# Second layer's modulation as VectorE row sums in the first feed-forward, in place of TensorE products in the recurrence

## The chip, the cores and the metric

One core of one Trainium2 chip. The time is device time in microseconds of one launch; its measurement for the kernel before is three runs, 1637.95, 1640.65 and 1649.41 us, median 1640.65 us.

Engines are called by the names of the profile: PE is TensorE (PEld its weight loads), DVE is VectorE, ACT is ScalarE, POOL is GpSimd, and SP is the engine whose queue issues most of the loads.

## The reference, cut to what matters

Two layers over 256 latent tokens of 1024 channels, with 256 context tokens beside them in the first layer. Each layer is half a feed-forward, a mixer, and half a feed-forward. All three are modulated: a vector `silu(c)` times a 1024 x 9216 matrix of the layer gives nine vectors of 1024 values, three (shift, scale, gate) for each of the three parts.

```python
m_lat = jnp.split((jax.nn.silu(c) @ ada_w[i] + ada_b[i])[:, None, :], N_MOD, axis=-1)
...
def half_ffn(h, m, off, g, w_gu, w_down):
    y = rmsnorm(h, g) * (1 + m[off + 1]) + m[off]
    return h + 0.5 * m[off + 2] * swiglu(y, w_gu, w_down)
...
h_lat = half_ffn(h_lat, m_lat, 0, norm_g[i, 0], ffn1_w_gu[i], ffn1_w_down[i])
y_lat = modulate(h_lat, norm_g[i, 1], m_lat[3], m_lat[4])
h_lat = h_lat + m_lat[5] * mixer(y_lat)
h_lat = half_ffn(h_lat, m_lat, 6, norm_g[i, 2], ffn2_w_gu[i], ffn2_w_down[i])
```

The first layer (i = 0) does the same for the context with `m_ctx` from `c_ctx`. Its mixer is RWKV-7, a recurrence over tokens with a 64 x 64 state for each of 12 heads and in both directions, beside a Fourier mixing of a quarter of the channels. The second layer's mixer is a gated depthwise convolution beside a pooling; the context takes no part in that layer.

## The kernel before, in words

**Tiles.** The tokens' state h lies with channels on partitions, as 8 tiles of 128 channels by 256 tokens for each stream. A weight of 128 x 1024 is loaded whole on SP's queue (tile `wraw`, 512 KB) and split into two parts, `whi` by ScalarE (L190) and `wlo` by VectorE (L191); each product is three matmuls (L195 to L197), high by high, high by low, low by high.

**Stages, in order.** The first feed-forward (`ffn`, both streams, 512 columns a product) runs until about 405 us: 22 slots in three parts of 8, 7 and 7, a slot being a gate and an up product of 8 x 3 matmuls each, the product of the two (`hd`, L433) and its low part (`hl`, L361). At a part's end come the 8 products of `down`, and after each the update of h. Gate and up products use four PSUM banks in turn, down products two. Then come the input projection of the mixer and its features, and from 551 us on the recurrence: three groups of four heads, for each group the generator `chain` with 8 steps of 64 tokens (four of the context, then four of the latent tokens, which also give outputs by L821 and L823). A step issues small products of 64 or 128 rows and columns, each waiting for the one before through VectorE, ScalarE or GpSimd. In between, six pieces at a time after each step (`PR[0]`), stands the work of the next group (`features`, `inverse`), or for the last group the Fourier mixing and most of the output projection (`project_most`). When that has run out, the chain's steps stand alone; this is from 605 us in the first group, from 743 in the second and from 872 in the third. After the recurrence follow three feed-forwards over the latent tokens alone and the second layer's mixer.

**The modulation of the first layer.** `ada_first` makes the first norm's columns on TensorE. All others, 56 columns of 128 values for the latent stream and 24 for the context, are row sums: `ada_job` loads two columns' weights, transposed, as a tile `adaw` of 128 x 2048 (L277, 1024 KB, on GpSimd's queue, three buffers), and VectorE multiplies it elementwise by `cb`, which holds silu(c) in every partition, and adds up along the free dimension in the same instruction (L281, `accum_out`). These jobs are a list of generators, and each slot of the first feed-forward, and each down product but the last part's last two, takes two steps of it (`jobs` = 2, 44 places in all); there are 60 steps.

**The modulation of the second layer.** `ada_wide` makes it on TensorE. Each of 18 blocks of 512 columns gets four loads of 512 KB on SP's queue, into the buffers of `wraw`, and eight matmuls with silu(c) as 32 stationary columns and 512 columns of weights (L260), four of them side by side in rows of 32 of one bank. Then a copy by ScalarE (`adas`, L265), four transposes (L268) and a reduction by VectorE (L269) into `mod[1, 0]`. The matmuls have a lowered priority for the scheduler (-200). In the recurrence, after each step of `chain`, 4, 5 or 4 pieces of this list are driven, by the group (`PR[1 + g]`). `mod[1, 0]` is read from the third feed-forward on.

**Order.** The order on each engine is made by a scheduler from the order of the program and these priorities; an engine runs its instructions in that order, and one that waits holds all behind it.

Of the kernel before, what the change touches and what calls it, by code (L numbers as in the profile page):

```python
# [7 lines left out]
F32 = mybir.dt.float32  # L8
F32R = mybir.dt.float32r
AF = mybir.ActivationFunctionType  # L10
ALU = mybir.AluOpType
# [36 lines left out]
def dft():  # L48
    """[bd(cos64) | bd(sin64)] / 128, then cos256 and -sin256 by tiles of rows."""
# [13 lines left out]
def pool_counts():  # L63
    """1 / tokens of the centred windows, by the widths of the four groups."""
    t = np.arange(T)
    z = np.zeros((P, 2, T), np.float32)
    for g, w in enumerate((2, 4, 8, 16)):
        n = np.minimum(t + w - 1 - w // 2, T - 1) - np.maximum(t - w // 2, 0) + 1
        z[g % 2 * CW:g % 2 * CW + CW, g // 2, :] = 1.0 / n
    return z  # L70
# [9 lines left out]
def lay_out(a):  # L80
    """Arrays of the launch: inputs re-laid so that every load is contiguous per partition."""
# [19 lines left out]
    d["adat"] = w[0].T.reshape(9 * KT // 2, 2, P, D)[KT:].transpose(0, 2, 1, 3)  # L101
    d["ada1"] = w[1].reshape(4, 2, P, 18, 512).transpose(3, 0, 2, 1, 4)
# [31 lines left out]
class Net:  # L134
# [76 lines left out]
    def ada_first(self, b, r, ab):  # L211
        """Shift and scale of channel tile b of the first norm, for both streams, into columns b of ab."""
# [20 lines left out]
    def ada_rows(self, pool, vecs):  # L233
        """silu(c) along the free dimension of every partition."""
# [13 lines left out]
    def ada_wide(self, b, pool):  # L248
        """Columns 512 b .. of the second layer's modulation, in pieces of four loads."""
        nc = self.nc  # L250
        ps = self.bank("ada")
        for q in range(4):
            w = self.wp.tile([P, KT, P], F32, tag="wraw", name=self.nm("wraw"), bufs=4)
            w = w.rearrange("p k c -> p (k c)").rearrange("p (k n) -> p k n", k=2)
            nc.sync.dma_start(w, self.ins["ada1"][b, q])
            for i in range(2):
                k = 2 * q + i
                g = k % 4
                with self.tc.high_priority(-200):
                    nc.tensor.matmul(ps[32 * g:32 * g + 32, :], lhsT=self.cs[:, k, :], rhs=w[:, i, :],  # L260
                                     start=k < 4, stop=k >= 4, tile_position=(0, 32 * g), skip_group_check=True)
                if i:
                    yield
        sb = self.mp.tile([P, 512], F32, tag="adas", name=self.nm("adas"), bufs=1)
        nc.scalar.copy(sb, ps)  # L265
        pt = self.bank("ada")
        for i in range(4):
            nc.tensor.transpose(pt[:, i * P:(i + 1) * P], sb[:, i * P:(i + 1) * P], self.ident)  # L268
        nc.vector.tensor_reduce(out=self.mod[1, 0][:, 4 * b:4 * b + 4], in_=pt.rearrange("p (b g v) -> p b v g", b=4, g=4)[:, :, 0, :],  # L269
                                axis=AX.X, op=ALU.add)  # L270
        yield

    def ada_job(self, blk, vecs):
        """Columns blk and blk + 1 of the first layer's modulation, as sums along the free dimension."""
        nc = self.nc
        w = self.ap.tile([P, KT, 256], F32, tag="ada0", name=self.nm("adaw"), bufs=3).rearrange("p (i a) b -> p i (a b)", i=2)
        nc.gpsimd.dma_start(w, self.ins["adat"][blk // 2 - KT])  # L277
        for i in range(2):
            for v in vecs:
                junk = self.ap.tile([P, D], F32, tag="adaj", name=self.nm("adaj"), bufs=1)  # L280
                nc.vector.scalar_tensor_tensor(out=junk, in0=w[:, i, :], scalar=1.0, in1=self.cb[v], op0=ALU.mult,  # L281
                                               op1=ALU.mult, accum_out=self.mod[0, v][:, blk + i:blk + i + 1])
# [5 lines left out]
    def modcol(self, l, v, m, scale=None, g=None):  # L288
        """Columns [P, KT] of modulation m; optionally scaled, or (1 + m) * g."""
# [1070 lines left out]
```

## Time and profile before

| | |
|---|---|
| median of three runs | 1640.65 us |
| the profiled execution (span) | 1651.6 us |
| PE busy | 1555.6 us, 94% |
| PEld busy | 1319.8 us, 80% |
| DVE busy | 1082.6 us, 66% |
| ACT busy | 677.3 us, 41% |
| POOL busy | 204.9 us, 12% |
| instructions | 29927 |
| moved by DMA | 253.40 MB |

The profiled execution has no other time than its span, and is one execution apart from the three runs. A share of busy time is a mean over stages that differ, so the views are read stage by stage: windows of time give each engine's busy time in a stretch, with the clock that TensorE was granted (1.00 is full speed) and the share of time in which the 16 DMA engines were busy; the chain of waits gives what the end of a stretch waited for, step by step; lines and timelines give single instructions.

### The profile page before, as it was taken

How to read it: one execution, taken by the hardware profiler on the slowest of the kernel's cores; microseconds unless marked ns; L12 is line 12 of the kernel's file. 1: busy time of each engine (PE TensorE's matmuls, PEld its weight loads, DVE VectorE, ACT ScalarE, POOL GpSimd, SP SyncE). 2: the span in 40 equal slices, each digit the busy share in tenths (PEclk: the TensorE clock that was granted, in tenths of full speed). 3: DMA queues.
4: the chain of work that ended last, by engine and by line, in shares of the span. 5: the costliest groups of instructions: out<-in, count | busy, mean ns of one | idle time of the engine just before them, and what ended most of it. 6: DMA issues, size and time to landing. Idle time of an engine off the chain costs nothing.

```text
span 1651.6 us, 29927 instructions
## 1 busy us (share of the span) xinstructions
PE 1555.6 (94%) x12102; PEld 1319.8 (80%) x12102; DVE 1082.6 (66%) x1994; ACT 677.3 (41%) x1101; POOL 204.9 (12%) x291
## 2 busy tenths in 40 slices
PE   5999999999989899899999899999999996899997
PEld 3788888888867655555587699999999985799997
DVE  4899954335689686466462577656776479767754
ACT  4431222223553542441441455444454355445442
POOL 0000100000040430330210100000000056300000
PEclk9999999999989789789995899999999997799999
DMA  9667943223222124444530355565556532435562
GB/s 370 230 242 257 346 136 103 95 84 123 77 65 96 56 93 151 158 170 148 191 104 14 116 180 186 175 187 179 181 182 176 167 102 89 141 130 185 181 177 95
DMA packets 68810, 253.40 MB, mean 153 GB/s; under 512 B 8032, under 2 KB 10864, under 8 KB 63936
## 3 DMA queue, kind: packets, MB, share of 16 engines
q1 hardware_dynamic: 64080, 219.46, 40.2%
q0 software_dynamic: 4592, 32.03, 5.4%
q8 instruction: 95, 1.56, 0.4%
q14 instruction: 43, 0.35, 0.1%
HBM read 249.36 MB, written 2.10 MB: 152 GB/s over the span
## 4 chain that ended last, share of the span: by engine, by line
PE 81%; DVE 13%; ACT 3%; issue 2%; POOL 1%; DMA 1%; SPq 0%; POOLq 0%; DVEq 0%; ACTq 0%
PE gu L195 13%; PE gu L196 13%; PE gu L197 13%; PE down L197 7%; PE down L195 7%; PE down L196 7%; PE ada L260 3%; PE mx L823 2%; PE mx L821 2%; DVE wlo L191 2%; DVE ocv L1022 1%; DVE oo L1022 1%; PE gu L1049 1%; PE pg L744 1%; PE down L802 1%
## 5 line engine op out<-in xcount | busy, mean ns | idle before, releaser
L190 ACT CAST whi<-wraw 128x1024 fp32r<-128x1024 f32 (+1 forms) x298 | 305.1, 1028 | 524.5 <-PE gu L196 224.0
L191 DVE TENSOR_TENSOR wlo<-wraw,whi 128x1024 fp32r<-128x1024 f32 (+1 forms) x298 | 356.6, 1199 | 154.0 <-ACT whi L190 146.4
L195 PE MATMUL gu<-yh,whi 128*128 128x258 f32 (+1 forms) x1408 | 438.4, 312 | 6.4 <-ACT yh L375 4.5
L196 PE MATMUL gu<-yl,whi 128*128 128x258 f32 (+1 forms) x1408 | 437.6, 311 | 0.0
L197 PE MATMUL gu<-yh,wlo 128*128 128x258 f32 (+1 forms) x1408 | 436.5, 310 | 0.2 <-DVE wlo L191 0.2
L195 PEld LDWEIGHTS gu<-yh,whi 128*128 128x128 f32 x1408 | 265.8, 189 | 24.2 <-ACT yh L375 5.7
L197 PEld LDWEIGHTS gu<-yh,wlo 128*128 128x128 f32 x1408 | 267.4, 190 | 15.2 <-DVE wlo L191 1.1
L196 PEld LDWEIGHTS gu<-yl,whi 128*128 128x128 f32 x1408 | 267.2, 190 | 14.8 <-DVE yl L377 0.9
L196 PE MATMUL down<-hl,whi 128*128 128x256 f32 (+1 forms) x704 | 217.3, 309 | 0.0
L195 PE MATMUL down<-hh,whi 128*128 128x256 f32 (+1 forms) x704 | 217.3, 309 | 0.0
L197 PE MATMUL down<-hh,wlo 128*128 128x256 f32 (+1 forms) x704 | 217.3, 309 | 0.0
L195 PEld LDWEIGHTS down<-hh,whi 128*128 128x128 f32 x704 | 134.4, 191 | 7.4
L197 PEld LDWEIGHTS down<-hh,wlo 128*128 128x128 f32 x704 | 134.4, 191 | 7.4
L196 PEld LDWEIGHTS down<-hl,whi 128*128 128x128 f32 x704 | 134.4, 191 | 7.3
L350 POOL TENSOR_TENSOR rs<-ms,mhalf 128x2 f32<-128x2 f32 (+1 forms) x9 | 10.9, 1209 | 822.8 <-DVE ms L347 822.8
L281 DVE SCALAR_TENSOR_TENSOR adaj<-adaw,cb 128x1024 f32<-128x1024 f32 x80 | 97.8, 1223 | 4.0 <-DMA adaw<-in_adat_dram 2.8
L260 PE MATMUL ada<-wraw,ccs 128*32 128x512 f32 x288 | 75.9, 669 | 1.0 <-DVE mod L269 1.0
L384 DVE SCALAR_TENSOR_TENSOR hlat<-down,mc,hlat 128x256 f32<-128x256 f32 x46 | 22.2, 483 | 62.9 <-PE down L197 62.9
L438 DVE COPY wb<-gu 128x1 f32<-128x1 f32 x132 | 20.3, 154 | 46.4 <-PE gu L197 46.4
L360 ACT CAST hh<-hd 128x256 fp32r<-128x256 f32 (+1 forms) x88 | 40.5, 461 | 23.9 <-DVE hd L433 13.1
L964 PE MATMUL gu<-yo,wraw 128*128 128x256 f32 x192 | 45.4, 396 | 1.9 <-ACT yo L375 1.9
L1006 POOL TENSOR_TENSOR opart<-opart,opr 128x256 f32<-128x256 f32 x54 | 45.2, 837 | 5.0 <-ACT opr L1004 1.2
(339 smaller groups left out, 2419.1 us busy)
## 6 DMA issues: line engine op xcount, KB each, us to landing
wraw<-in_gu_dram SPq DMA_DIRECT2D x176, 512.0 KB, 3.3
wraw<-in_ada_dram SPq DMA_DIRECT2D x72, 512.0 KB, 4.2
adaw<-in_adat_dram POOLq DMA_DIRECT2D x28, 1024.0 KB, 5.7
wraw<-in_down_dram SPq DMA_DIRECT2D x64, 448.0 KB, 3.3
wraw<-in_down_dram SPq DMA_DIRECT2D x32, 512.0 KB, 3.5
wraw<-in_win_dram SPq DMA_DIRECT2D x22, 512.0 KB, 3.5
wraw<-in_owin_dram SPq DMA_DIRECT2D x14, 512.0 KB, 3.6
ada<-in_ada_dram SPq DMA_DIRECT2D x4, 1024.0 KB, 16.8
```

The source lines that it names most:

```text
L190: nc.scalar.copy(hi[:, :k, :], raw[:, :k, :])
L191: (eng or nc.vector).tensor_tensor(out=lo[:, :k, :], in0=raw[:, :k, :], in1=hi[:, :k, :].bitcast(F32), op=ALU.subtract)
L195: mm(ps, lhsT=wh, rhs=xh, start=start, stop=False, **k)
L196: mm(ps, lhsT=wh, rhs=xl, start=False, stop=False, **k)
L197: mm(ps, lhsT=wl, rhs=xh, start=False, stop=stop, **k)
L260: nc.tensor.matmul(ps[32 * g:32 * g + 32, :], lhsT=self.cs[:, k, :], rhs=w[:, i, :], start=k < 4, stop=k >= 4, tile_position=(0, 32 * g), ...
L281: nc.vector.scalar_tensor_tensor(out=junk, in0=w[:, i, :], scalar=1.0, in1=self.cb[v], op0=ALU.mult, op1=ALU.mult, accum_out=self.mod[0, v ...
L360: self.nc.scalar.copy(hi, x)
L821: mm(p3[o:o + CW, x, :], lhsT=UV[:, x, hd, :], rhs=rv(S["RR"][:, hd, x, :]), start=True, stop=False, tile_position=(0, o), skip_group_chec ...
L823: mm(p3[o:o + CW, x, :], lhsT=Xs[lo, x, hd, :], rhs=rv(r), start=False, stop=True, tile_position=(0, o), skip_group_check=True)
L964: nc.tensor.matmul(ps[:, :n], lhsT=w[:, k, :], rhs=y[:, k, :], start=k == 0, stop=k == KT - 1)
L1006: nc.gpsimd.tensor_tensor(out=part, in0=prev, in1=pr, op=ALU.add)
```

## The change

The second layer's 72 columns are computed like the first layer's: 36 more jobs on the same list, for the latent stream alone, each a load of 1024 KB on GpSimd's queue and two row sums on VectorE. The list has 132 steps, and each of the 44 places takes three. `ada_wide` goes, and with it its loads, matmuls, copies, transposes and reductions and the driving of it in the recurrence. The launch lays out both layers' weights transposed in one array. The diff also drops docstrings and comments, which are left out here; lines move by 1 to 28 numbers.

```diff
-    d["adat"] = w[0].T.reshape(9 * KT // 2, 2, P, D)[KT:].transpose(0, 2, 1, 3)
-    d["ada1"] = w[1].reshape(4, 2, P, 18, 512).transpose(3, 0, 2, 1, 4)
+    d["adat"] = w.transpose(0, 2, 1).reshape(9 * KT, 2, P, D)[KT:].transpose(0, 2, 1, 3)
...
-    def ada_wide(self, b, pool):
...
-    def ada_job(self, blk, vecs):
+    def ada_job(self, l, blk, vecs):
         nc = self.nc
         w = self.ap.tile([P, KT, 256], F32, tag="ada0", name=self.nm("adaw"), bufs=3).rearrange("p (i a) b -> p i (a b)", i=2)
-        nc.gpsimd.dma_start(w, self.ins["adat"][blk // 2 - KT])
+        nc.gpsimd.dma_start(w, self.ins["adat"][l * 9 * KT // 2 + blk // 2 - KT])
         for i in range(2):
             for v in vecs:
                 junk = self.ap.tile([P, D], F32, tag="adaj", name=self.nm("adaj"), bufs=1)
                 nc.vector.scalar_tensor_tensor(out=junk, in0=w[:, i, :], scalar=1.0, in1=self.cb[v], op0=ALU.mult,
-                                               op1=ALU.mult, accum_out=self.mod[0, v][:, blk + i:blk + i + 1])
+                                               op1=ALU.mult, accum_out=self.mod[l, v][:, blk + i:blk + i + 1])
             yield
...
-PR = (6,4,5,4)
+PR = 6
...
-                    net.jobs += [net.ada_job(m * KT + k, (0, 1) if m < 5 else (0,)) for m in range(2, 9) for k in range(0, KT, 2)]
+                    net.jobs += [net.ada_job(0, m * KT + k, (0, 1) if m < 5 else (0,)) for m in range(2, 9) for k in range(0, KT, 2)]
+                    net.jobs += [net.ada_job(1, k, (0,)) for k in range(0, 9 * KT, 2)]
...
-                    net.ffn(0, h, yh, yl, gate, acc, fp, 2, start)
+                    net.ffn(0, h, yh, yl, gate, acc, fp, 3, start)
...
-            wide = [net.ada_wide(b, lp) for b in range(18)]
...
-                    drive(side, PR[0])
-                    drive(wide, PR[1 + g])
+                    drive(side, PR)
...
-            drive(wide, 1000)
```

The order on VectorE in the first feed-forward, between the fourth and the fifth gate product (`hd`) of the second part. Before:

```order
L433 TENSOR_TENSOR hd_1630<-sg_1629,gu_1604 128x512
L191 TENSOR_TENSOR wlo_1790<-wraw_1791,whi_1789 128x1024
L361 TENSOR_TENSOR hl_1338<-hd_1630,hh_1337 128x512
L191 TENSOR_TENSOR wlo_1821<-wraw_1822,whi_1820 128x1024
L433 TENSOR_TENSOR hd_1704<-sg_1703,gu_1678 128x512
```

The same place after (L407 is `hd`, L190 `wlo`, L335 `hl`, L255 a row sum, `mc` columns of the first layer's gate):

```order
L407 TENSOR_TENSOR hd_1690<-sg_1689,gu_1664 128x512
L190 TENSOR_TENSOR wlo_1860<-wraw_1861,whi_1859 128x1024
L335 TENSOR_TENSOR hl_1386<-hd_1690,hh_1385 128x512
L255 SCALAR_TENSOR_TENSOR adaj_1777,mod_77<-adaw_1775,cb 128x1024
L255 SCALAR_TENSOR_TENSOR adaj_1779,mod_77<-adaw_1775,cb 128x1024
L255 SCALAR_TENSOR_TENSOR adaj_1851,mod_77<-adaw_1849,cb 128x1024
L190 TENSOR_TENSOR wlo_1891<-wraw_1892,whi_1890 128x1024
L255 SCALAR_TENSOR_TENSOR adaj_1853,mod_77<-adaw_1849,cb 128x1024
L255 SCALAR_TENSOR_TENSOR adaj_1857,mod_77<-adaw_1855,cb 128x1024
L266 TENSOR_TENSOR mc_1876_10574<-mod_77,smallc 128x8
L255 SCALAR_TENSOR_TENSOR adaj_1933,mod_77<-adaw_1855,cb 128x1024
L407 TENSOR_TENSOR hd_1768<-sg_1767,gu_1742 128x512
```

Before, the row sums have ended by this place; after, six of them stand here, and such a run stands between most gate products until the fifth of the last part's seven, ahead of which the last row sum stands.

The order on TensorE in the recurrence, at the second latent step of the first group: L823 the last output product of the step before, L782, L791 and L730 (transposes of values) the step's own products, L260 and L268 the second layer's modulation. Before:

```order
L823 MATMUL mx_5589<-rs_5312,Xs_5510 64x64
L782 MATMUL down_5629<-XV_5281,AG_5543 64x64
L260 MATMUL ada_5238<-wraw_5489,ccs 32x512
L260 MATMUL ada_5238<-wraw_5493,ccs 32x512 x2
L782 MATMUL down_5629<-XV_5281,AG_5543 64x64 x7
L268 MATMUL ada_5499<-cst,adas_5497 128x128 x4
L791 MATMUL down_5640<-RH_5638,A_3316 64x64 x8
L730 MATMUL mx_5664<-cst,z_3298 128x128
```

The same place after (L797, L756, L704 and L765 are the lines 823, 782, 730 and 791 of before):

```order
L797 MATMUL mx_5705<-rs_5469,Xs_5646 64x64
L756 MATMUL down_5728<-XV_5438,AG_5679 64x64 x8
L704 MATMUL mx_5763<-cst,z_3514 128x128
L704 MATMUL mx_5763<-cst,vr_5765 128x128
L704 MATMUL mx_5763<-cst,z_3694 128x128
L704 MATMUL mx_5763<-cst,vr_5769 128x128
L765 MATMUL down_5739<-RH_5737,A_3532 64x64 x8
```

The modulation's products and transposes are gone from the step, and the transposes of values (L704) now stand ahead of the product by the inverse (L765) and not behind it.

## Rows read from the trace of the kernel before

**Rows 1.** The page: the chain that ended last, by line.

```profile
PE gu L195 13%; PE gu L196 13%; PE gu L197 13%; PE down L197 7%; PE down L195 7%; PE down L196 7%; PE ada L260 3%; PE mx L823 2%; PE mx L821 2%; DVE wlo L191 2%; DVE ocv L1022 1%; DVE oo L1022 1%; PE gu L1049 1%; PE pg L744 1%; PE down L802 1%
```

**Rows 2.** The chain by line, in 551.2 to 828.5, 605 to 651.2, 743 to 787.6.

```profile
by line: PE ada L260 20.7%; PE mx L823 6.0%; PE mx L821 5.8%; PE down L802 4.3%; PE down L782 4.0%; PE misc L629 3.7%; PE pg L744 3.7%; PE down L791 3.5%; PE ada L268 3.2%; PE mx L763 3.2%; PE misc L648 2.7%; issue 2.5%; POOL inv L560 1.8%;
...
by line: PE ada L260 24.8%; PE mx L823 18.3%; PE mx L821 18.0%; PE down L782 7.1%; PE pg L744 6.9%; PE down L791 5.3%; PE down L802 3.7%; PE mx L763 3.0%; PE ada L268 2.7%; ACT XV L732 2.5%; PE pg L741 2.4%; ACT UV L733 2.1%; PE mx L730 1.3
...
by line: PE ada L260 19.8%; PE mx L823 17.3%; PE mx L821 16.5%; PE pg L744 7.2%; PE ada L268 5.5%; PE down L802 4.9%; ACT adas L265 4.0%; PE down L791 4.0%; DVE Z L666 3.2%; DVE sub L664 3.0%; PE down L782 2.5%; DVE mc L292 2.1%; PE mx L730
```

**Rows 3.** Windows of the recurrence: stretch, us, busy by engine, PEclk, DMA share, GB/s.

```profile
551.20:828.50 277.30, 258.81 (x3067) 153.76 (x3066) 176.55 (x388) 111.61 (x218) 74.16 (x101) 0.88 0.42 145
605.00:651.20 46.20, 45.89 (x449) 28.36 (x449) 30.07 (x80) 9.09 (x25) 4.97 (x6) 0.93 0.39 131
743.00:787.60 44.60, 42.57 (x400) 26.16 (x399) 30.43 (x80) 8.18 (x23) 4.13 (x5) 0.92 0.45 161
866.00:872.60 6.60, 6.60 (x54) 5.62 (x52) 2.27 (x4) 0.15 (x1) 0.00 (x0) 1.00 0.26 82
873.90:889.40 15.50, 14.82 (x106) 11.07 (x106) 4.47 (x8) 4.02 (x11) 1.05 (x1) 0.50 0.00 1
889.40:903.10 13.70, 13.70 (x97) 10.46 (x97) 3.63 (x6) 1.31 (x6) 1.05 (x1) 0.50 0.00 0
903.10:912.40 9.30, 8.29 (x64) 6.16 (x63) 2.74 (x7) 0.75 (x2) 1.05 (x1) 0.50 0.01 2
```

**Rows 4.** Windows of the first feed-forward, all engines; last, L281 on VectorE alone.

```profile
57.40:216.90 159.50, 158.28 (x690) 128.96 (x689) 153.83 (x255) 48.02 (x57) 13.25 (x25) 1.00 0.76 270
216.90:342.30 125.40, 125.40 (x549) 102.59 (x548) 45.13 (x57) 32.41 (x40) 0.00 (x0) 1.00 0.31 99
342.30:405.50 63.20, 62.16 (x316) 52.30 (x314) 28.22 (x49) 19.75 (x34) 2.29 (x3) 1.00 0.28 87
186.00:206.00 20.00, 20.00 (x90) 16.41 (x89) 18.91 (x31) 6.45 (x8) 2.67 (x6) 1.00 0.96 355
...
57.40:216.90 159.50, 98.47 (x160) 1.00 0.76 270
```

**Rows 5.** Lines of the whole span: count, busy us, mean ns, idle before and releaser.

```profile
L260 PE MATMUL ada<-wraw,ccs 128*32 128x512 f32 x288 | 75.9, 669 | 1.0 <-DVE mod L269 1.0
L268 PE MATMUL ada<-cst,adas 128*128 128x128 f32 x72 | 12.9, 302 | 2.6 <-ACT adas L265 2.6
```

**Rows 6.** Windows of the small-product steps: L260 alone (PE, PEld), then L268 alone.

```profile
605.00:651.20 46.20, 11.96 (x48) 1.62 (x48) 0.93 0.39 131
743.00:787.60 44.60, 11.41 (x49) 1.50 (x49) 0.92 0.45 161
...
605.00:651.20 46.20, 1.34 (x9) 0.87 (x9) 0.93 0.39 131
743.00:787.60 44.60, 2.43 (x12) 1.55 (x12) 0.92 0.45 161
```

**Rows 7.** VectorE's timeline: start, us, instruction, in brackets the idle time before it.

```profile
185.48 0.68 DVE L433 TENSOR_TENSOR hd<-sg,gu 128x512 f32<-128x512 f32 x1
...
196.32 0.68 DVE L433 TENSOR_TENSOR hd<-sg,gu 128x512 f32<-128x512 f32 x1
...
202.03 1.23 DVE L281 SCALAR_TENSOR_TENSOR adaj<-adaw,cb 128x1024 f32<-128x1024 f32 x1 [0.88 <-DMA adaw<-in_adat_dram]
...
208.12 0.68 DVE L433 TENSOR_TENSOR hd<-sg,gu 128x512 f32<-128x512 f32 x1
...
342.33 0.69 DVE L433 TENSOR_TENSOR hd<-sg,gu 128x512 f32<-128x512 f32 x1 [3.38 <-PE gu L197]
```

**Rows 8.** GpSimd's timeline: first and last of twelve loads of the row sums.

```profile
161.53 0.53 POOL L277 DMA_DIRECT2D adaw<-in_adat_dram  x1 [2.04 <-DVE adaj L281]
...
205.84 0.53 POOL L277 DMA_DIRECT2D adaw<-in_adat_dram  x1 [3.87 <-DVE mc L292]
```

**Rows 9.** The page: DMA issues, count, KB each, median us from issue to landing.

```profile
adaw<-in_adat_dram POOLq DMA_DIRECT2D x28, 1024.0 KB, 5.7
```

More of the change, by code (lines that the diff above doesn't have):

```diff
@@ L246, in ada_rows_job @@
         yield
-    def ada_wide(self, b, pool):
[L250 to L271, printed above, removed]
-    def ada_job(self, blk, vecs):
+    def ada_job(self, l, blk, vecs):
         nc = self.nc
         w = self.ap.tile([P, KT, 256], F32, tag="ada0", name=self.nm("adaw"), bufs=3).rearrange("p (i a) b -> p i (a b)", i=2)
-        nc.gpsimd.dma_start(w, self.ins["adat"][blk // 2 - KT])
+        nc.gpsimd.dma_start(w, self.ins["adat"][l * 9 * KT // 2 + blk // 2 - KT])
         for i in range(2):
```

## The prediction

> **What bounds the kernel now.** I read the chain of waits first, then the same chain by stage, then busy time and granted clock by stage, then single lines. Over the whole span the chain runs on TensorE, in the three-product lines of the feed-forwards; the modulation's products (L260) hold 3% of it [rows 1]. That is little of the whole but much of one place: within 551.2 to 828.5 us, the recurrence of groups 0 and 1, L260 holds 20.7% and its transposes (L268) 3.2% of the chain [rows 2]. 23.9% of 277.3 us is 66 us. There TensorE is busy 258.81 of 277.30 us at a mean clock of 0.88 and VectorE 176.55 [rows 3]: TensorE's queue, served in order, bounds the stage, and the wide products stand in it. The first feed-forward is bound by TensorE as well: in 216.9 to 342.3 it is busy all the time, VectorE only 45.13 of 125.40 us and DMA 31%; but in 57.4 to 216.9, where the first layer's row sums run, VectorE is busy 153.83 of 159.50 us [rows 4].
>
> The sum is made on the profiled execution, whose span of 1651.6 us is the only time that it has; it lies 11 us above the median of the three runs (1640.65), so the difference is put on that median.
>
> **What leaves the recurrence.** 288 pieces of product, 75.9 us busy, and 72 of transpose, 12.9 us [rows 5, 6]: 88.8 us, of which 66 lie on the chain; the rest filled gaps. With them go the 18 ScalarE copies, the 18 VectorE reductions and SP's 72 loads of these weights; none of these bounds the stage, and I count them at nothing. That they go is no loss for another load, since SP's queue there only gets shorter.
>
> What is late next? I split the stage in two.
>
> First the small-product steps, 605 to 651.2 and 743 to 787.6, 90.8 us together [rows 3]. L260 and L268 hold 27.5% and 25.3% of the chain there [rows 2]: 12.7 + 11.3 = 24 us. At an unchanged clock they would take 66.8 us. But the same four steps run in group 2 without the wide products, and there the rows show something else: from 873.9 on, TensorE is busy 14.82 of 15.50, then 13.70 of 13.70 us, granted 0.50, the 1.2 GHz level, and the three steps take 15.5, 13.7 and 9.3 us [rows 3]. With one more of 13.7, four steps are 52.2 us, against 46.2 and 44.6 now. So between 66.8 and 104.4 us; up to 872.6, with the projection's products between those of the recurrence, the row shows 1.00, the 2.4 GHz level [rows 3]; it fell when these had ended and the recurrence ran alone. I take the middle, 85.6, since each of the new stretches begins behind feature products with 512 columns and should start warm: a gain of 5 us.
>
> Then the rest of the stage, 186.5 us, with features, inverse and output of the heads. On its chain stand 66 - 24 = 42 us of L260 and L268. Taking them away can cost something only by the clock, so the bounds are 42 gained and, all at 1.2 GHz, 2 lost (worked out under the second rival). VectorE, ScalarE and GpSimd steps of the features come to stand on the path where TensorE stood, and the clock, at about 0.86 there now, falls somewhat: I take two thirds, 28 us.
>
> Stage: 33 us gained, between 66 gained and 16 lost.
>
> **What the first feed-forward gets.** 36 loads of 1024 KB on GpSimd's queue and 72 row sums on VectorE, three steps of the list per slot instead of two; 152 row sums in all. In the order they end ahead of the fifth of the last part's seven gate products, where before the 80 end in the middle part. That product is read at 342.33 now [rows 7].
>
> VectorE: 80 row sums are busy 98.47 us, 1.231 us each [rows 4] (the row counts 160, with the read of each sum's accumulator). Up to 342.3 it has 153.83 + 45.13 - 98.47 = 100.5 us of other work; with 152 x 1.231 = 187.1 this makes 287.6 in 284.9 us. Full, and 3 us over, without a gap. Loads: the row sums of one stream ran with a load issued each 4.03 us (161.53 to 205.84, eleven steps) [rows 8], and VectorE waited for them at times (0.88 us at 202.03) while two slots took 10.84 and 11.80 us [rows 7]. That was at a DMA share of 0.96, 355 GB/s [rows 4]. 36 more loads at that pace end at 205.84 + 36 x 4.03 = 351; with a landing of 5.7 [rows 9] and two row sums the last is done at 359, 17 us behind the 342.3.
>
> How much of 17 us does TensorE pay? The gate and up products have four banks, two slots, so some 11 us of lateness pass unseen within a part; VectorE is idle in 35 of the 63.2 us behind it [rows 4] and catches up. At the end of a part it is otherwise: the down products need the last hl at once, and each update frees one of two banks. There a few us are paid, at the first and the second part. The nearest row for the whole is today's stretch at the same load, where TensorE was busy 20.00 of 20.00 us [rows 4], so nothing lost in 45 us; it now lasts four times as long. Bounds: nothing, and 25 us (all 17, and 8 for weights that land late). I take 10, nearer to the row. What waits: each new load on GpSimd's queue waits for the sums that read its buffer; behind it stand only further loads, then the power of the norm, long after. A row sum that waits for its load holds hd, hl, the updates and the low weight parts behind it on VectorE; the low parts run several weights ahead, the others are what TensorE feels. The second layer's columns are used only after 940 us, so nobody waits for the results.
>
> **Sum.** -33 + 10 = -23: 1640.65 - 23 = 1617.6, say 1618 us. Group 2 and all behind it I cost at nothing: the projection's weights may land earlier once the wide loads have left SP's queue, the order there changes little.
>
> **Rivals.** (1) The whole share on the chain falls off: -66, with 5 for the feed-forward: 1580 us. It holds if the clock stays. The Trainium skill, page "TensorE: Matmul & The Clock Gate", section on the clock gate, has the clock follow how busy the engine has been, with 1.2 GHz as the idle state; by it, steps as full as these would stay at 2.4 GHz. The row at 889.4, full and at 0.50, speaks against that.
> (2) Slower: without wide products the recurrence stays at 1.2 GHz. The small steps cost 104.4 - 90.8 = 13.6 more. In the rest TensorE has 170.4 us busy [rows 3], less 61.6 of L260 and L268 (88.8 less 27.1) [rows 5, 6]: 109. At a clock of 0.86, and with 52.2 against 33.4 us for the price of the lower level (1.56), 109 is 98 us of work at 2.4 and 153 at 1.2 GHz: 44 more, against the 42 gained. Together 16 lost, and 10 in the feed-forward: 1667 us. It decides once two thirds of the way from "as now" to "all at 1.2 GHz" are gone: 66 - 10 = 56 of 82 us. For it: group 2's rows. Against: feature products and the 32-row products of the inverse, between which the clock was up again.
> (3) The feed-forward becomes bound by loads and VectorE, +25: 1633 us. For it: 355 GB/s at a share of 0.96. The Trainium skill, page "DMA: Bandwidth & Descriptors", section "Issuing engines are not separate DMA queues", says that loads from all queues share the same engines; by that GpSimd's queue gives the row sums no room of their own and SP's weights land later. The share agrees.
> (4) The change does what it says, but features and substitution set the recurrence: only 15 of 66 gained, 1636 us. VectorE's 176.55 of 277.3 leaves room, so I give it little.
>
> **How the numbers follow.** Forecast 0.50, with its own range 1600 to 1632; rival 1 0.13, 2 0.13, 3 0.14, 4 0.10. A measurement of this kernel tells about 1% from no change, that is 1624 and 1657 as marks. Faster by over 1%: 0.45 of the forecast and rival 1, 0.58. Within: 0.05 of the forecast, 0.12 of rival 3 and rival 4, 0.27. Slower: rival 2 and the rest of 3, 0.15. The range 1585 to 1650 leaves out most of rivals 1 and 2.
>
> **What would show it.** Right: the recurrence of groups 0 and 1 some 33 us shorter, with a granted clock of 0.7 to 0.8 there and rows of 0.50 in the small steps; VectorE over 95% busy from 62 to about 350; short TensorE gaps at the ends of the first two parts, the first feed-forward 10 us longer. Wrong: a clock of 0.88 or more there with 60 us gained, 0.6 with none; or a first feed-forward longer by over 20 or not at all.

## The result, and the profile after

The changed kernel takes 1652.25 us (median of 20 runs, 1639.65 to 1660.62) against 1639.41 us before (20 runs, 1634.84 to 1653.14). The ratio is 1.0055, with a 95% interval from 1.0031 to 1.0079; it goes by all runs, whose means (1649.8 and 1641.0 us) lie 9 us apart, and not by the medians, which lie 13 apart. That is slower by half a per cent where 23 us less were forecast, and outside the range. Two executions in a slow state (2076.72 us at a clock of 0.635 with the paced sums below, and 1880.29 us at 0.734 of the kernel before beside the spread jobs) are in no ratio.

The profiled execution of before (span 1651.6 us) is among the longest of its twenty; that of the changed kernel is 1650.3 us long, near its median. The two traces differ by 1 us where the medians differ by 13, so a few us between them prove little; where several traces can be compared below, they are.

The page of the changed kernel, busy time and the chain by line:

```profile
PE 1523.9 (92%) x11742; PEld 1334.4 (81%) x11742; DVE 1156.4 (70%) x2120; ACT 666.9 (40%) x1083; POOL 220.5 (13%) x327
...
PE gu L194 10%; PE gu L195 10%; PE gu L196 10%; PE down L195 6%; PE down L196 6%; PE down L194 6%; DMA adaw<-in_adat_dram 3%; PE mx L795 2%; PE mx L797 2%; DVE wlo L190 2%; PE gu L938 1%; PE gu L1023 1%; PE pg L718 1%; PE down L756 1%; DVE oo L996 1%
```

The wide products (3% of [rows 1]) are gone from the chain, and TensorE's busy time is 32 us less. But 88.8 us of it were taken out [rows 5], so what is left must have become longer by 57 us.

**The recurrence.** Its first mark is the first copy of `RH` (a tile that each step of `chain` makes once) by ScalarE, at 553.1 us before and 563.1 after; its second the same copy in the third group, at 802.7 and 797.3; its end the first update of h, at 930.6 and 932.1. Windows of the kernel before, whole recurrence (us, busy time of PE, PEld, DVE, ACT, POOL, granted clock, DMA share, GB/s):

```profile
553.10:930.60 377.50, 351.94 (x3751) 226.79 (x3747) 221.34 (x476) 137.57 (x268) 85.64 (x112) 0.84 0.35 122
```

The same of the changed kernel; the two rows above the last are its two halves:

```profile
563.10:797.30 234.20, 199.11 (x2231) 147.92 (x2227) 148.49 (x314) 84.45 (x166) 64.79 (x87) 0.61 0.03 8
797.30:932.10 134.80, 118.99 (x1148) 92.71 (x1148) 62.86 (x130) 44.12 (x84) 21.09 (x25) 0.76 0.16 50
563.10:932.10 369.00, 318.10 (x3378) 240.64 (x3374) 211.35 (x443) 128.57 (x249) 85.88 (x112) 0.67 0.08 23
```

Read the last row against that of before. In the window of before L260 and L268 are busy 74.8 and 12.9 us, 87.7 together (two of the 288 products stand ahead of it). TensorE is now busy 318.1 us with what took 351.9 - 87.7 = 264.2 us; the clock has gone from 0.84 to 0.67. Its idle time is 50.9 us, where it was 25.6. So the account of the recurrence is -87.7 for the work removed, +53.9 for the rest at a lower clock, and +25.3 of idle time, most likely waits that the wide products had covered: -8.5 us. That these three add up is no proof, since busy and idle time always do; what shows the clock's part are the fillers below.

The three steps between the fifth and the eighth `RH` of the first two groups, where small products stand nearly alone, answer to the small-product rows of [rows 3]. Before:

```profile
607.40:641.80 34.40, 34.09 (x332) 22.00 (x334) 23.23 (x56) 7.80 (x23) 3.92 (x5) 0.90 0.29 96
742.10:781.60 39.50, 37.59 (x342) 22.93 (x342) 26.30 (x65) 7.75 (x22) 4.13 (x5) 0.91 0.39 135
```

After:

```profile
621.30:655.80 34.50, 31.65 (x296) 24.01 (x296) 20.87 (x54) 6.05 (x19) 4.15 (x6) 0.71 0.01 2
744.70:783.70 39.00, 35.82 (x296) 27.43 (x296) 23.28 (x55) 8.17 (x21) 4.08 (x6) 0.59 0.05 15
```

73.9 us became 73.5: the steps lost their wide products and are as long as before.

**The first feed-forward.** From the first gate product (`hd`) to the last update of h it is 350.8 us long, 342.3 before. TensorE's timeline shows where (start, us, instruction, in brackets the idle time before it and what ended it):

```profile
253.04 0.39 PE L196 MATMUL down<-hh,wlo 128*128 128x512 f32 x1
259.67 0.80 PE L194 MATMUL down<-hh,whi 128*128 128x512 f32 x1 [6.25 <-ACT hh L334]
```

VectorE's timeline in the same place:

```profile
257.13 1.23 DVE L255 SCALAR_TENSOR_TENSOR adaj<-adaw,cb 128x1024 f32<-128x1024 f32 x1 [1.73 <-DMA adaw<-in_adat_dram]
...
258.29 0.68 DVE L407 TENSOR_TENSOR hd<-sg,gu 128x512 f32<-128x512 f32 x1
```

At the end of the second part the down products need the last `hh` (the high part of `hd`), that needs the last `hd`, and between this `hd` and the one before it stand six row sums on VectorE, the last of which waits 1.73 us for its load. Row sums have waited for loads ahead of this, too: 8.8 us up to here and 13.7 in the whole feed-forward, for 2.8 before. TensorE stands idle for 6.25 us, once. The product behind the gap takes 0.80 us and not 0.39: the idle time has brought the clock to the lower level, 1.2 GHz. That stretch in a window:

```profile
257.50:264.40 6.90, 4.57 (x12) 3.32 (x13) 6.87 (x12) 1.56 (x2) 0.53 (x1) 0.56 0.83 292
```

The eight products from 259.67 on take 4.0 us to issue, and 1.9 at the pace ahead of the gap. So 6.25 us of gap and some 2 us behind it are the 8.5 us of the feed-forward.

How long the gap is differs from execution to execution: in the four other traces below with all 36 jobs placed by the scheduler and loaded it is 1.41 to 3.83 us, and the feed-forward is 4.0 to 7.4 us longer than before. The mean of the five is 6.2 us, and the 8.5 here is their upper end.

### The profile page after: what moved, and what is told of

Same layout as the page of the kernel before. It is cut to its first block, busy times and chain, and to the rows that moved or that the text cites. A ratio compares the mean times of both kernels' runs of the same rounds, so it can differ in the third digit from the quotient of the medians.

```text
span 1650.3 us, 29269 instructions
## 1 busy us (share of the span) xinstructions
PE 1523.9 (92%) x11742; PEld 1334.4 (81%) x11742; DVE 1156.4 (70%) x2120; ACT 666.9 (40%) x1083; POOL 220.5 (13%) x327
## 4 chain that ended last, share of the span: by engine, by line
PE 69%; DVE 13%; issue 9%; DMA 4%; ACT 2%; POOL 2%; SPq 0%; POOLq 0%; DVEq 0%; ACTq 0%
PE gu L194 10%; PE gu L195 10%; PE gu L196 10%; PE down L195 6%; PE down L196 6%; PE down L194 6%; DMA adaw<-in_adat_dram 3%; PE mx L795 2%; PE mx L797 2%; DVE wlo L190 2%; PE gu L938 1%; PE gu L1023 1%; PE pg L718 1%; PE down L756 1%; DVE oo L996 1%
## 5 line engine op out<-in xcount | busy, mean ns | idle before, releaser
L190 DVE TENSOR_TENSOR wlo<-wraw,whi 128x1024 fp32r<-128x1024 f32 (+1 forms) x298 | 356.2, 1198 | 121.3 <-ACT whi L189 113.7
L255 DVE SCALAR_TENSOR_TENSOR adaj<-adaw,cb 128x1024 f32<-128x1024 f32 x152 | 185.4, 1220 | 15.0 <-DMA adaw<-in_adat_dram 13.7
L196 PEld LDWEIGHTS down<-hh,wlo 128*128 128x128 f32 x704 | 134.8, 191 | 7.3
L251 POOL DMA_DIRECT2D adaw<-in_adat_dram x64 | 33.9, 529 | 288.2 <-DVE adaj L255 202.7
L334 ACT CAST hh<-hd 128x256 fp32r<-128x256 f32 (+1 forms) x88 | 40.4, 460 | 68.0 <-DVE hd L407 57.4
```

Source lines behind the costliest of these rows:

```text
L190: (eng or nc.vector).tensor_tensor(out=lo[:, :k, :], in0=raw[:, :k, :], in1=hi[:, :k, :].bitcast(F32), op=ALU.subtract)
L196: mm(ps, lhsT=wl, rhs=xh, start=False, stop=stop, **k)
L251: nc.gpsimd.dma_start(w, self.ins["adat"][l * 9 * KT // 2 + blk // 2 - KT])
L334: self.nc.scalar.copy(hi, x)
```

## The experiments

Twelve kernels were run. First the two halves of the change, each alone, and two that put back on TensorE work like that taken from it, without its use (the fillers). The recurrence alone (the 36 jobs of the second layer are left out, so this kernel doesn't compute that modulation):

```diff
-                    net.jobs += [net.ada_job(1, k, (0,)) for k in range(0, 9 * KT, 2)]
+                    nc.vector.memset(net.mod[1, 0], 0.0)
...
-                    net.ffn(0, h, yh, yl, gate, acc, fp, 3, start)
+                    net.ffn(0, h, yh, yl, gate, acc, fp, 2, start)
```

> The changed kernel without the second layer's 36 jobs (that modulation is left out and set to zero), two steps a slot as before: the recurrence without wide products, alone. Theory (clock): in the recurrence the 66 us of wide products came back through the lower granted clock, and the +9 us of the changed kernel is the first feed-forward's; then this takes 1639 to 1645 us, as before, with a granted clock near 0.62 from the first to the last step of groups 0 and 1. Rival (the feed-forward hides a gain): if the recurrence had gained the forecast 33 us, 1606. Rival (features, substitution and the chain of small products set the stage at any clock): also about 1640, but with a clock above 0.8.

Measured: 1639.12 us (12 runs), ratio to before 0.9999 (0.9974 to 1.0023). Its recurrence:

```profile
551.90:919.00 367.10, 313.49 (x3380) 238.44 (x3376) 211.30 (x443) 128.60 (x250) 87.18 (x112) 0.68 0.07 23
```

Taking 66 us off the chain of the recurrence is worth nothing here, within some 4 us either way, and it isn't the feed-forward that hides a gain.

The feed-forward alone (to the kernel before, with both layers' weights transposed in `adat`):

```diff
+                    net.jobs += [net.ada_job(2, k, (0,)) for k in range(0, 9 * KT, 2)]
...
-                    net.ffn(0, h, yh, yl, gate, acc, fp, 2, start)
+                    net.ffn(0, h, yh, yl, gate, acc, fp, 3, start)
```

> The kernel before with the 36 loads and 72 row sums added to the first feed-forward, three steps a slot; their results go to a tile that nobody reads, and the wide products stay in the recurrence. Theory: +9 us, 1648, as one gap of some 6 us of TensorE at the end of the second part, with a stretch at 0.50 behind it; the recurrence as before, clock 0.85 to 0.93. Rival (loads hidden): 1640. Rival (feed-forward costs more in the median than in the profiled execution): 1655.

Measured: 1649.40 us (6 runs), ratio 1.0074 (1.0055 to 1.0093): the whole loss of the change. In its profiled execution the gap at the end of the second part was 2.6 us and the first feed-forward 347.1 us long, 4.8 more than before, so this trace shows less than half of the 12 us; where the others lie it doesn't show. This is also a second trace of the recurrence with wide products:

```profile
561.00:930.90 369.90, 343.58 (x3749) 220.46 (x3746) 221.65 (x477) 137.38 (x267) 84.09 (x112) 0.87 0.35 125
```

With the products the recurrence took 377.5 and 369.9 us; without them it took, in the five traces of this study without fillers and the one with tiny fillers, 366.3 to 374.8, 370.0 in the mean. The gain is some 4 us; the 8.5 of the first two traces lie above it.

Eight fillers after each step of the changed kernel's recurrence, then four:

```diff
+    def fill(self, n):
+        ps = self.bank("ada")
+        for i in range(n):
+            g = i % 4
+            with self.tc.high_priority(-200):
+                self.nc.tensor.matmul(ps[32 * g:32 * g + 32, :], lhsT=self.cs[:, i % KT, :], rhs=self.cst[:, :512],
+                                      start=True, stop=True, tile_position=(0, 32 * g), skip_group_check=True)
...
                     drive(side, PR)
+                    net.fill(8)
```

> The changed kernel with eight matmuls of 32 stationary and 512 moving columns after each step of the recurrence, on constants that are there already: as many and as wide as the products that were taken out, without loads, copies, transposes or reductions, and with no result that anybody reads. Theory (clock): the granted clock of groups 0 and 1 comes back from 0.62 to 0.85 or more, and what the fillers take is given back by it, so that the time stays within 10 us of the changed kernel's, 1640 to 1655. Rival (the stage is bound by waits on the other engines at any clock): fillers cost about two thirds of the 76 us that such products took, 1700, or, where they only fill gaps, nothing, with no change of the other products' durations.

One number in it is wrong: the wide products were 144 matmuls (288 instructions, [rows 5]), the fillers of all groups are 288 (576 instructions). Measured: 1645.87 us (6 runs), ratio 1.0053 (1.0032 to 1.0074). Its recurrence, and in the second fence L252, the fillers, alone (PE and PEld):

```profile
563.60:921.60 358.00, 345.44 (x3936) 199.26 (x3935) 214.95 (x445) 127.13 (x249) 80.43 (x112) 0.95 0.08 26
```

```profile
563.60:921.60 358.00, 116.69 (x552) 17.11 (x552) 0.95 0.08 26
```

More work on the engine that bounds the stage, and the stage is 11 us shorter than without it: the clock is 0.95, and the products of use take 345.4 - 116.7 = 228.7 us, not 318.1. The first two groups are 222.2 us long (234.2 without fillers), the third is no shorter. A bound by waits on other engines at any clock is excluded. The whole gained less: 6.6 of the 11 us are lost behind the recurrence (724.8 us from its end to that of the span, for 718.2), and the ratio, 1.0053, is that of the changed kernel. Why the stretch behind is longer is not shown.

> The same with four fillers after each step. Theory (clock): if half of them hold the clock nearly as high (0.8), the recurrence is shorter than with eight or none: 1620 to 1640. If the clock goes by the share of such products, it is about 0.73 and the time between that of eight and of none. Rival (bound by waits on other engines): 1675 or no change.

Measured: 1650.91 us (6 runs), ratio 1.0071 (1.0046 to 1.0097): clock 0.95 in the first group, 0.85 in the second, 0.75 and 0.72 in the third, recurrence 373.4 us; no filler stands in the third. That is no better than eight; the expected optimum wasn't there.

Then the feed-forward's gap. The second layer's sums on a tile that is there already (this kernel leaves out the loads, and so the second layer's modulation):

```diff
         nc = self.nc
-        w = self.ap.tile([P, KT, 256], F32, tag="ada0", name=self.nm("adaw"), bufs=3).rearrange("p (i a) b -> p i (a b)", i=2)
-        nc.gpsimd.dma_start(w, self.ins["adat"][l * 9 * KT // 2 + blk // 2 - KT])
+        if l:
+            w = self.cbt
+        else:
+            w = self.ap.tile([P, KT, 256], F32, tag="ada0", name=self.nm("adaw"), bufs=3).rearrange("p (i a) b -> p i (a b)", i=2)
+            nc.gpsimd.dma_start(w, self.ins["adat"][blk // 2 - KT])
```

> The changed kernel with the second layer's 72 row sums in place and order, but reading a tile that is there already: their 36 loads are left out, and their results are not the modulation. Theory (late sums hold the end of the second part because the loads set their pace, a megabyte each 4 us at a DMA share of 0.96): the gap of 6 us before the down products of the second part goes, the first feed-forward is back to its length of before within 2 us, and the time about 9 us under the changed kernel's, 1641. Rival (VectorE itself is full, 287 us of work in 285): the gap stays, 1650.

Measured: 1646.28 us (10 runs, 1633.8 to 1653.14), ratio 1.0022 (0.9989 to 1.0054); in the trace the gap is gone and the first feed-forward is 343.5 us long, 1.2 more than before. VectorE has room for 152 sums; it is the wait for loads that costs. The total is too scattered to confirm 1641.

The jobs spread over three feed-forwards (12 in each, in the later two with two buffers shared with later tiles and the sums written in place):

```diff
-                    net.jobs += [net.ada_job(1, k, (0,)) for k in range(0, 9 * KT, 2)]
+                    net.jobs += [net.ada_job(1, k, (0,)) for k in range(0, 24, 2)]
...
-        half_ffn(0, 2, 1)
-        half_ffn(1, 0, 2)
+        half_ffn(0, 2, 1, 1, range(24, 48, 2))
+        half_ffn(1, 0, 2, 1, range(48, 72, 2))
```

> The changed kernel with the second layer's jobs spread: 12 in the first feed-forward (two steps a slot, as before), 12 in the second, 12 in the third, there with two buffers and sums written in place. Theory: the second and third feed-forward have room on VectorE (about 70% busy) and on the DMA engines (45%), so that the row sums cost nothing and this equals the recurrence without products alone: 1636 to 1643, a ratio to the kernel before of 1.00. Rival (there they delay the low weight parts, as in the first): 1650 or more.

Measured: 1655.33 us (6 runs), ratio 1.0102 (1.0063 to 1.0141), and with fillers driven in groups 0 and 1:

> The same with eight fillers of 512 columns, in float32, after each step of groups 0 and 1 alone. The run with eight in all three groups had the first steps of group 0 to those of group 2 in 222 us, against 234 in the changed kernel and 250 before, and group 2 as long with fillers as without. Theory (clock): 1640 less 10 to 12, 1626 to 1632, with a clock above 0.9 in groups 0 and 1. Rival (what is gained there is lost later, at lower clock behind it): 1640.

1642.21 us (12 runs), ratio 1.0017 (0.9994 to 1.0041). Its recurrence is 353.1 us long, that of the spread jobs alone 374.8. Both missed by things that the traces show. TensorE's waits in the first feed-forward of the spread jobs, and a window in the second feed-forward:

```profile
258.60 0.80 PE L194 MATMUL down<-hh,whi 128*128 128x512 f32 x1 [5.64 <-ACT hh L344]
```

```profile
950.00:1060.00 110.00, 108.27 (x903) 108.09 (x902) 104.77 (x207) 58.23 (x84) 8.03 (x18) 1.00 0.88 314
```

A third of the jobs in the first feed-forward makes about the gap that all of them made in the changed kernel, and in the third feed-forward no load of them is left: from 1150 to 1260 us the DMA share is 0.55 and VectorE is busy 79.9 us, where the changed kernel has 0.59 and 80.0. In the second, TensorE is busy 108.27 of 110 us, where the changed kernel has all 110, and behind the recurrence the trace of the spread jobs, the longest of their six executions, takes 730.4 us for 718.2. The number of steps per slot doesn't set where the sums stand: they crowd together at the front. The reading is that the scheduler takes each as early as it believes its load to have landed; what it believes is in no trace.

Fillers in bfloat16, one instruction each:

```diff
+                self.nc.tensor.matmul(ps[32 * g:32 * g + 32, :], lhsT=self.fb[:, :32], rhs=self.fb,
```

> The changed kernel with eight fillers after each step in bfloat16, 512 columns, on a constant tile. A float32 filler is two matmul instructions of 0.64 us in the trace; one in bfloat16 is one instruction, so this is at most half the time of fillers of the run with eight in float32, on as many places. Theory A (the clock goes by how long TensorE is busy): clock between those of four in float32 (0.95 and 0.85 in groups 0 and 1) and of none (0.63 and 0.59), time 1640 to 1650. Theory B (it goes by the kind of work, wide against small products, and few suffice): clock as with eight, 0.94, and a time under 1640, since the fillers take less.

Measured: 1649.48 us (10 runs), ratio 1.0051 (1.0021 to 1.0081), clock 0.90 and 0.66 in groups 0 and 1 (four in float32: 0.95 and 0.85; none: 0.63 and 0.59), 36.0 us of fillers. The scheduler moved most of them forward: of 288 instructions 213 (28.3 us) run by the end of group 0, 79 (7.7 us) in group 1 and none in group 2. In group 0 they are more instructions than those of four in float32 (144), but take less time (38.4 us there), and they hold the clock less, which speaks for theory A and against B; in group 1 there are too few to try B. The recurrence is 361.5 us long, 7.5 less than in the changed kernel, and the ratio as there.

Last, the order of the sums is made to follow the program, and fillers are added to that:

```diff
+                if l:
+                    self.tc.keep_in_program_order(m)
...
-                    net.ffn(0, h, yh, yl, gate, acc, fp, 3, start)
+                    net.ffn(0, h, yh, yl, gate, acc, fp, 4, start)
```

with `m` the row sum, and two steps in a down slot.

> The changed kernel with the second layer's 72 row sums held in the order of the program on VectorE (each behind what stands before it there), four steps of the list in a gate slot and two in a down slot, instead of as early as the scheduler takes their loads to have landed. No work is left out. Theory (what costs 9 to 12 us in the first feed-forward is the row sums' place ahead of the last gate product of the second part, where they wait for loads): the gap of 6 us and the stretch at half clock behind it go, the time is that of the run without these jobs: 1637 to 1643. Rival (the loads as such or VectorE's fill cost it): 1648 to 1652.

Measured: 1648.96 us (11 runs), ratio 1.0056 (1.0028 to 1.0084). The gap at the end of the second part is gone and the first feed-forward is 344.4 us long, 6.4 less than in the changed kernel; 3 us are lost ahead of it, where TensorE now waits 4.1 us for a first `sg` (1.2 before), and the recurrence of this execution, 373.4 us, takes the rest. The theory of the place holds by the stage; the total didn't fall to 1643. Order and steps per slot were changed at once; that fewer steps alone leave the gap is what the spread jobs show.

> The same with eight float32 fillers after each step of groups 0 and 1. From the run of spread jobs with fillers (1642) come off the gap of 5.5 us with its half clock in the first feed-forward, 9, and some 4 lost in the later feed-forwards: 1629, between 1622 and 1634, below the kernel before (1640). Rival (what fillers gain is lost in the executions with a long tail): 1640.

Measured: 1631.94 us (6 runs, 1631.30 to 1637.20), ratio 0.9952 (0.9937 to 0.9967): faster than before by half a per cent, and than the changed kernel by 20 us in the medians and 17 by the ratios. Its recurrence, and group 1 of it:

```profile
560.90:914.00 353.10, 331.23 (x3773) 208.27 (x3771) 215.66 (x445) 127.97 (x250) 79.35 (x112) 0.89 0.08 24
...
666.70:783.00 116.30, 112.22 (x1448) 61.91 (x1448) 77.70 (x156) 45.85 (x89) 30.89 (x44) 0.94 0.05 16
```

Group 1 of the paced sums alone:

```profile
655.00:787.60 132.60, 109.09 (x1244) 82.35 (x1244) 79.27 (x169) 46.09 (x88) 33.02 (x44) 0.56 0.03 10
```

The same products, one line of them with fillers and then without (count, busy us, mean ns):

```profile
L775 PE MATMUL down<-RH,A 64*64 64x64 f32 x128 | 5.9, 225 | 0.4 <-ACT A L684 0.3
...
L767 PE MATMUL down<-RH,A 64*64 64x64 f32 x128 | 9.3, 308 | 1.6 <-ACT RH L761 1.6
```

In group 1 the fillers (200 instructions) are busy 41.4 us. The work of use is busy 112.2 - 41.4 = 70.8 us at 0.94 and 109.1 at 0.56, 38 us less, and the idle time 4.1 us, for 23.5; against the fillers' 41.4 us this makes 16.3. In group 0 nothing is gained by time (105.8 us, for 99.9), although the clock there is 0.95 and not 0.73. Group 2, with hardly a filler, is 9.9 us shorter (131.0, clock 0.80, for 140.9, clock 0.72).

The kernel does all the work of the changed one, and 192 matmuls that nobody reads.

> The same with twelve fillers. If eight already hold the clock (0.95), four more cost their time on the chain of groups 0 and 1: 96 more matmuls at two instructions of some 0.4 us each, half of them in gaps, +20 to +40 over eight fillers. If the clock still rises, within 5 us of eight.

Measured: 1649.53 us (6 runs), ratio 1.0064 (1.0039 to 1.0089), 17.6 us over eight. Group 0 holds no more fillers than with eight (166 instructions for 174) and has the same clock, 0.95. The added ones stand in group 1 (313 for 200) and behind it: group 1 takes 142.1 us for 116.3, at a clock of 0.90 for 0.94. What is added beyond eight is only paid for; why the clock of group 1 is lower with more of them is not shown.

A control, with fillers of 8 columns:

```diff
-                self.nc.tensor.matmul(ps[32 * g:32 * g + 32, :], lhsT=self.cs[:, i % KT, :], rhs=self.cst[:, :512],
+                self.nc.tensor.matmul(ps[32 * g:32 * g + 32, :8], lhsT=self.cs[:, i % KT, :], rhs=self.cst[:, :8],
```

> The run with paced row sums and eight fillers, with 8 columns in a filler in place of 512: as many instructions in about the same places, with next to no work. Theory (the fillers act through the clock alone): the clock of groups 0 and 1 falls back to 0.6 to 0.7, the first steps of group 0 to those of group 2 take 232 us again (222 with full fillers), and the time is that of paced row sums without fillers, 1645 to 1652. Rival (fillers help by another order of the instructions on TensorE): 1632, and 222 us.

Measured: 1649.63 us (12 runs), ratio 1.0067 (1.0038 to 1.0096). Its groups 0 and 1 together, the whole recurrence, and the fillers alone in group 0 and in group 1:

```profile
559.20:791.00 231.80, 197.00 (x2587) 149.10 (x2586) 149.14 (x315) 84.25 (x165) 64.45 (x87) 0.66 0.03 8
...
559.20:925.50 366.30, 315.13 (x3735) 241.58 (x3734) 211.88 (x445) 128.41 (x249) 85.58 (x112) 0.70 0.07 23
...
559.20:662.80 103.60, 9.05 (x346) 6.54 (x346) 0.73 0.02 4
662.80:791.00 128.20, 0.00 (x0) 0.00 (x0) 0.59 0.03 11
```

As many instructions without the work leave the clock at 0.66 and the first two groups at 231.8 us. But they don't stand in the same places, as was expected: the scheduler has all 384 of them run between 557.1 and 603.7 us, in group 0 and just ahead of it, and none in group 1. So the control holds for group 0 alone: there the instructions as such leave the clock at 0.73, where those with work hold 0.95. In group 1, where most of the time of the stage is gained, it says nothing of another order of the instructions. There the case for the clock is the one above, that equally many products take less time each, 225 ns for 308, at a granted clock of 0.94 for 0.56. A control with tiny fillers held in group 1 was not run.

## Why the prediction was wrong

**What leaves the recurrence** was counted rightly: 88.8 us busy, and 66 on the chain by the view. The idle time of TensorE grew by 25.3 us, close to the 22.8 that were said to fill gaps.

**The clock's price is the step that failed.** The forecast let 33 of the 66 us come back; in the two traces 57.5 did (66 less 8.5), and by the runs all of it within 4 us (0.9999 for the recurrence alone). In two terms the lower clock was priced too low. For the small-product steps "I take the middle, 85.6 [...] a gain of 5 us": three of each four of them show 73.9 and 73.5 us, no gain. For the rest of the stage "I take two thirds, 28 us": its clock did not fall "somewhat" from 0.86 but to 0.61 over both groups. The clock is that of the mark that the prediction itself set for being wrong, 0.6 with nothing gained. Groups 0 and 1 did become shorter, from 249.6 to 234.2 us where 33 us were forecast, but some 250 products of theirs have moved behind the boundary to group 2, and of the whole recurrence 4 us are left in the mean of the traces.

What could have been read: the price of a clock. Product of TensorE's useful busy time and clock in the recurrence, over five kernels:

| kernel | busy, less wide or fillers, us | clock | product |
|---|---|---|---|
| before | 264.2 | 0.84 | 222 |
| changed | 318.1 | 0.67 | 213 |
| eight fillers | 228.7 | 0.95 | 217 |
| paced, eight fillers | 331.2 - 80.8 = 250.4 | 0.89 | 223 |
| paced, tiny fillers | 315.1 - 9.1 = 306.0 | 0.70 | 214 |

The work is some 217 us at 2.4 GHz, and busy time is that over the clock, within 3%; the other traces give 211 to 225, the low ones where the clock is low. The prediction took 1.56 as the price of the lower level. Its 33.4 us were steps at a clock of 0.92 to 0.93 and not at 2.4 GHz, with other limits beside the clock; by these rows TensorE's busy time, though not its idle time, nearly doubles. And the clock goes with the work that TensorE has: in group 0 fillers of 512 columns hold it at 0.95, as many of 8 columns leave it at 0.73; in group 1 it is 0.94 with fillers and 0.56 to 0.59 without. "Busy" in the profile doesn't tell this, since an engine at half clock looks fuller: it was busy 199 of 234 us at 0.61.

The Trainium skill, page "TensorE: Matmul & The Clock Gate", section on the clock gate, has the clock follow how busy the engine has been. The runs with fillers agree in direction (0.67 without, 0.95 with eight after each step); that steps as full as these would by it stay at 2.4 GHz, as rival 1 had it, is denied by the row of 13.70 us busy in 13.70 at 0.50 [rows 3].

**Group 2 at nothing**: its part, from 802.7 to 930.6 us before, is 127.9 us long, 134.8 after; the boundary holds more work after (1148 matmul records against 936), so the whole recurrence is what counts above.

**The first feed-forward** came about as forecast: +10 predicted, +8.5 in the trace of the change, 4.0 to 8.5 in five traces and 12 by the runs of the feed-forward alone, paid at the end of a part by `hd` behind row sums that wait for loads. The gap is at the second part's end alone, not the first's, and a quarter of the 8.5 is the clock behind the gap, which the sum didn't have. The fifth gate product of the last part is read at 356.73 us, 14.4 later than before, for 17 forecast. The row that the prediction read as nothing lost in 45 us covers 20 of them; from 57.4 to 216.9 us TensorE was idle for 1.2 us even before [rows 4]. VectorE is busy 94% of 62 to 350 us, for over 95 forecast.

**The rivals.** Rival 1 (full gain) is out by the clock and the time, rival 4 (features and substitution bound the stage) by the fillers: a shorter stage with more work on TensorE. Rival 2 was right in its mechanism; in groups 0 and 1 the clock went two thirds of the way from 0.87 to 0.50, which is where the prediction had put the point of balance of the whole change. In the two traces it did balance: -8.5 in the recurrence, +8.5 in the feed-forward. In the runs the recurrence alone is even and the feed-forward's loss remains. Rival 3's +25 wasn't reached.

What stays open is why single executions differ by 20 us (1639.65 to 1660.62): the clock over a whole run goes with it, 0.914 at 1639.99 us and 0.895 at 1656.33 us, but what decides it from run to run no run here shows. The recurrence alone has it too (1632.58 to 1649.14). Open is also why gains by stage don't add up in the runs: three kinds of fillers beside the unpaced sums (1.0053, 1.0071, 1.0051) and paced sums without fillers (1.0056) all stay at the ratio of the changed kernel, 1.0055, and only both together come to 0.9952.

## What to carry to other kernels

Before work is taken off TensorE in a stage of small dependent products, read the granted clock there and multiply it with the busy time: if what is removed is what keeps the clock up, the rest gets longer, and here it took back all but some 4 of 66 us. Work that looks like a cost on the chain may be worth its place; if it goes, something else has to hold the clock, and the right amount is found by trying (beside paced sums eight fillers gained 17 us over none, twelve nothing; beside unpaced ones eight in all groups gained nothing in the runs). Where fillers stand is to be read from the trace, since a scheduler may move them. Sums that wait for loads belong behind what the next product needs, by an order held by hand where the scheduler puts them too early.

## What was not expected

- 192 matmuls without use, 80.8 us of TensorE's busy time, make the recurrence shorter: 353.1 us against 373.4 with paced sums alone, and against 366.3 to 374.8 in all six traces without such work.
- One gap of 6.25 us in a stage that is busy throughout halves the clock behind it: a product of 512 columns takes 0.80 us in place of 0.40, and 4 us pass until it takes 0.39 again.
- Fillers driven after each step don't stay there: all 384 instructions of 8 columns ran by the middle of the first group, and of those in bfloat16 213 of 288 by its end.
- Loads counted per slot don't stay there: 12 of 36 jobs in the first feed-forward leave a gap of 5.6 us, all 36 one of 1.4 to 6.25.
